# The final norm of the second half of a sequence, done by rows: tiles turned on TensorE behind the last product, the factor as a scalar of each partition

## The chip, the cores and the metric

The kernel runs on one core of one Trainium2 chip. The metric is the device time of one execution in microseconds (us). Engines are named as in the profile: PE is TensorE (PEld its weight loads), DVE is VectorE, ACT is ScalarE, POOL is GpSimd, SP is SyncE, which here only issues DMA transfers.

## What is computed

A decoder layer over 512 positions of 1024 channels: a gated feed-forward block, a mixer of sparse attention and a gated recurrence, a second feed-forward block, each behind an RMS norm and added to the running sum x; then one last RMS norm. The change is in the last block's down projection and in that last norm.

```python
def rmsnorm(x, g):
    x32 = x.astype(jnp.float32)
    y = x32 * lax.rsqrt(jnp.mean(x32 * x32, axis=-1, keepdims=True) + EPS)
    return (y * g.astype(jnp.float32)).astype(x.dtype)

def swiglu(x, w_gate, w_up, w_down):
    return (jax.nn.silu(x @ w_gate) * (x @ w_up)) @ w_down

# ... the last steps of the layer and of the whole:
        x = x + 0.5 * swiglu(rmsnorm(x, ffn2_norm[l]), ffn2_wg[l], ffn2_wu[l], ffn2_wd[l])
    return rmsnorm(x, final_norm)
```

All arrays are float32; the inner width of the feed-forward block is 2816.

## The kernel before

The running sum stands in SBUF turned: eight tiles x[0] to x[7] of 128 channels (partitions) by 512 positions. So a sum over channels goes over partitions and over the eight tiles, and the norm's factor is one number for each column.

A float32 product is made of three products of rounded parts (`mm3`): the high part of the weight with the high and the low part of the activations, and the low part of the weight with the high part. Weight tiles come by DMA as `wr` (queue of SP), ACT rounds them to `wh`, DVE subtracts to get `wl` (`wload`). In a name such as mm<-hh,wh the first tile is written (mm and aux are the two sets of four PSUM buffers each), the second streams through PE, the third stands in it.

`ffn_down` makes x[0] to x[6]: for each, 22 tiles of the hidden layer in three weight chunks (`CHUNKS`: 7, 7 and 8), 66 products over 512 positions, then DVE adds half of the PSUM sum to x[n], and `done(n)` squares it on ACT into `sq` and adds that to `acc` on DVE. For n of 2 and 5 POOL multiplies x[n] in place by the final gain, a column of `vt`.

x[7] is written out by hand behind it. The first two chunks (14 hidden tiles) go over all 512 positions; the last chunk (8 hidden tiles) goes over the two halves of the positions one after the other, `products(0, ...)` and `products(1, ...)`. `squares(h)` adds a half to x[7] and squares it into `last`. `norm_steps` makes the norm's factor for two blocks of 128 positions: PE multiplies `acc` and `last` (standing) with a constant `mean` (streaming), so that the mean square of a position stands on a partition; ACT takes the root (`sd`), DVE the reciprocal (`rs`, one column for each block); PE turns that column, spread over 128 columns, back to a row for all partitions, and ACT copies it to `rstd`. `finish(h, k)` multiplies tile k of a half with the gain's column and with `rstd`: on DVE for k of 0, 1, 3, 4, 6, 7, on POOL for 2 and 5, where the gain is in it already. SP sends the results out, in five transfers for each half (128, 256, 256, 256, 128 KB), in runs of 1 KB.

The order of these last steps on each engine is the order in which they are written (`tc.manual_schedule`). All that goes through the recording helpers carries line L174 in the profile, and all transfers line L162; so the rows are told apart by tile names. L1434 is the end of the program, where every engine drains and waits for the others: four engines count themselves in, POOL counts, and sends all of them on.

Of the kernel before, what the change touches and what calls it, by code (L numbers as in the profile page):

```python
# [9 lines left out]
F32 = mybir.dt.float32  # L10
F32R = mybir.dt.float32r
AF = mybir.ActivationFunctionType
ALU = mybir.AluOpType

P = 128
S = 512
D = 1024
KD = D // P
DFF = 2816
KF = DFF // P  # L20
# [3 lines left out]
QB = 128  # L24
NQ = S // QB
# [8 lines left out]
CHUNKS = ((0, 7), (7, 14), (14, 22))  # L34
# [9 lines left out]
WARM = 8  # L44
HS = S // 2
LEAD = 4
DIRECT = 4


# [6 lines left out]
V_G1, V_GM, V_G2, V_GF = 0, 8, 16, 24  # L56
# [120 lines left out]


@with_exitstack
def hybrid_kernel(ctx, tc, xt, vec, w1u, w1d, wm, wki, wrg, watt, wrnn, wout, w2u, w2d, out):  # L180
    nc = tc.nc
    plan = Plan()
    V, A = plan.engine("DVE", nc.vector), plan.engine("ACT", nc.scalar)
    G, T = plan.engine("POOL", nc.gpsimd), plan.engine("PE", nc.tensor)
    Q = plan.engine("SP", nc.sync)
# [9 lines left out]
    small = ctx.enter_context(tc.tile_pool(name="small", bufs=4))  # L195
# [6 lines left out]
    def nm(s):  # L202
        cnt[0] += 1
        return f"{s}_{cnt[0]}"

    def slot(dt=F32, name="s"):
        return plan.take("slot", big.tile([P, S], dt, tag="slot", name=nm(name)))

    def work(name="t", cols=S):
        return plan.take("tmp", tmp.tile([P, cols], F32, tag="tmp", name=nm(name)))  # L210
# [4 lines left out]
    def psum(tag="mm"):  # L215
        return psp.tile([P, S], F32, tag=tag, name=nm(tag))

    def psaux():
        return psum("aux")

    vt = const.tile([P, NV], F32, name="vt")
    x = [resid.tile([P, S], F32, name=f"x{k}") for k in range(KD)]
    ident = const.tile([P, P], F32, name="ident")
    mean = const.tile([P, P], F32, name="mean")
    epst = const.tile([P, 1], F32, name="epst")
    acc = resid.tile([P, S], F32, name="acc")
    rstd = resid.tile([P, S], F32, name="rstd")

    def col(base, k):
        return vt[:, base + k:base + k + 1]  # L230

    WMAX = KD * P
    def wtiles(cols):
        r = raw.tile([P, WMAX], F32, tag="raw", name=nm("wr"))[:, :cols]
        h = wsp.tile([P, WMAX], F32R, tag="wh", name=nm("wh"))[:, :cols]
        l = wsp.tile([P, WMAX], F32R, tag="wl", name=nm("wl"))[:, :cols]
        return r, h, l

    def wsplit(r, h, l):
        A.activation(h, r, AF.Copy)  # L240
        V.tensor_sub(l, r, f(h))

    def wload(src, cols):
        r, h, l = wtiles(cols)
        Q.dma_start(r, src)
        wsplit(r, h, l)
        return h, l

    def mm3(ps, w, c, y, start, stop):
        h, l = w  # L250
        yh, yl = y
        T.matmul(ps, h[:, c], yh, start=start, stop=False)
        T.matmul(ps, h[:, c], yl, start=False, stop=False)
        T.matmul(ps, l[:, c], yh, start=False, stop=stop)

    def gemm(ps, w, ys, ks, first=True, last=True, m=P, since=0, upto=None):
        n = len(ks)
        for i, k in list(enumerate(ks))[since:upto]:
            mm3(ps, w, slice(i * m, (i + 1) * m), ys[k], first and i == 0, last and i == n - 1)
# [28 lines left out]
    def waits(which, *tiles, aux=0, att=0, slots=0, key=None, mm=0, tmps=0):  # L288
        return which, tiles, aux, att, slots, key, mm, tmps

    def norm_steps(*sums, blocks=range(NQ)):
        pc, n = psaux(), len(blocks)
        for i, a in enumerate(sums):
            if i:
                yield waits("PE", a)
            for j, b in enumerate(blocks):

                T.matmul(pc[:, j * QB:(j + 1) * QB], a[:, b * QB:(b + 1) * QB], mean, start=i + j == 0,
                         stop=i == len(sums) - 1 and j == n - 1)
        yield waits("ACT", pc)  # L300
        sd = small.tile([P, NQ], F32, tag="st", name=nm("sd"))[:, :n]
        A.activation(sd, pc.rearrange("p (b c) -> p b c", c=QB)[:, :n, 0], AF.Sqrt, bias=epst)
        yield waits("DVE", sd)
        rs = small.tile([P, NQ], F32, tag="m8", name=nm("rs"))[:, :n]
        V.reciprocal(rs, sd)
        yield waits("PE", rs)
        pb = psaux()[:, :n * QB]
        for j in range(n):
            T.transpose(pb[:, j * QB:(j + 1) * QB], rs[:, j:j + 1].to_broadcast([P, P]), ident)
        yield waits("ACT", pb)  # L310
        A.activation(rstd[:, blocks[0] * QB:(blocks[-1] + 1) * QB], pb, AF.Copy)

    def norm_rest(steps):
        for _ in steps:
            pass

    lo, hi = slice(0, HS), slice(HS, S)
# [62 lines left out]
    def ffn_up(y, wu, n0, hs, g, waiting=(), given=()):  # L380
# [7 lines left out]
        H = KD // 2 * P  # L388
        f0 = n0 + DIRECT
        count = KF - f0  # L390
# [33 lines left out]
        def together(*steps):  # L424
            steps = list(steps)
            while steps:
                for i in list(steps):
                    try:
                        next(i)
                    except StopIteration:  # L430
                        steps.remove(i)
# [95 lines left out]
        with tc.manual_schedule(engines=ENGINES):  # L527
# [32 lines left out]
            for i in range(len(stream)):  # L560
# [3 lines left out]
                else:  # L564
                    together(results_direct(len(direct) - 1))
                if i + LEAD < len(stream):
                    prepare(i + LEAD)
                else:
                    halve(hs, f0 + i + LEAD - len(stream))
                if i % 14 == 12 and i // 14 < f0:  # L570
# [52 lines left out]
    for k in range(KD):  # L623
        if k:
            Q.dma_start(x[k], xt[k])
        if k % CH == 0:
            c = slice(k * P, (k + CH) * P)
# [14 lines left out]
    for k in range(KD):  # L642
        y.append(norm_tile(k, V_G1, False))
        if k % CH == 0:
            c = slice(k * P, (k + CH) * P)
# [4 lines left out]
    pu, w = psum(), given(AH[0])  # L650
# [3 lines left out]
    hs = []  # L654
# [5 lines left out]
    z, e, s_, s2 = (zt[:, 8 * i:8 * i + 8] for i in range(4))  # L660
# [646 lines left out]
    hs = []  # L1307
    ffn_up(y2, w2u, 0, hs, V_G2)

    def done(n):  # L1310
        sq = acc if n == 0 else work("sq")
        square(n, sq, A)
        if n:
            V.tensor_add(acc, acc, sq)
        if n % 3 == 2:
            G.tensor_scalar(x[n], x[n], col(V_GF, n), 0.0, op0=ALU.mult, op1=ALU.add)

    ffn_down(hs, w2d, done, KD - 1)

    n, e = KD - 1, x[KD - 1]
    po = psum()
    for a, b in CHUNKS[:-1]:
        w = wload(w2d[n, :, a * P:b * P], (b - a) * P)
        gemm(po, w, hs, range(a, b), first=a == 0, last=b == CHUNKS[-1][0])
    V.scalar_tensor_tensor(e, po, 0.5, e, op0=ALU.mult, op1=ALU.add)
    a, b = CHUNKS[-1]
    w = wload(w2d[n, :, a * P:b * P], (b - a) * P)
    last = work("last")  # L1330
    halves = [slice(h * S // 2, (h + 1) * S // 2) for h in range(2)]
    steps = []
    for h in range(2):
        steps.append(norm_steps(acc, last, blocks=(2 * h, 2 * h + 1)))
        next(steps[h])
    pos = [psum()[:, :S // 2] for _ in halves]

    def products(h, i, j):
        for k in range(a + i, min(a + j, b)):
            mm3(pos[h], w, slice((k - a) * P, (k - a + 1) * P), [t[:, halves[h]] for t in hs[k]], k == a, k == b - 1)  # L1340

    def squares(h):
        c = halves[h]
        V.scalar_tensor_tensor(e[:, c], pos[h], 0.5, e[:, c], op0=ALU.mult, op1=ALU.add)
        V.tensor_mul(last[:, c], e[:, c], e[:, c])

    def finish(h, k):
        c = halves[h]
        if k % 2 or k == 0:
            o[h] = slot(F32, "o")  # L1350
        oc = o[h].rearrange("p (k c) -> p k c", k=2)
        dst = oc[:, 1 - k % 2, :]
        if k % 3 == 2:
            G.tensor_mul(dst, x[k][:, c], rstd[:, c])
        else:
            V.scalar_tensor_tensor(dst, x[k][:, c], col(V_GF, k), rstd[:, c], op0=ALU.mult, op1=ALU.mult)
        if k in (0, KD - 1):
            Q.dma_start(out[k][:, c], dst)
        elif k % 2 == 0:
            Q.dma_start(out[k - 1:k + 1, :, c].rearrange("k p c -> p k c"), oc)  # L1360

    o = {}
    with tc.manual_schedule(engines=ENGINES):
        products(0, 0, b)
        squares(0)
        products(1, 0, 3)
        next(steps[0])
        next(steps[0])
        next(steps[0])
        products(1, 3, 5)  # L1370
        next(steps[0])
        norm_rest(steps[0])
        products(1, 5, b)
        finish(0, 0)
        squares(1)
        for k in range(1, 5):
            finish(0, k)
        next(steps[1])
        next(steps[1])
        next(steps[1])  # L1380
        norm_rest(steps[1])
        for k in range(5, KD):
            finish(0, k)
        for k in range(KD):
            finish(1, k)


def _tiles(w, kt, m=P):
# [49 lines left out]
```

## Time and profile before

| | |
|---|---|
| time, median of 3 runs | 1103.74 us (1102.88 to 1103.88) |
| time of the profiled execution | 1102.85 us |
| its span, first to last instruction | 1101.1 us |
| granted TensorE clock, mean | 0.995 |
| busy | PE 98%, PEld 86%, DVE 69%, ACT 54%, POOL 9% |
| read from and written to memory | 130.24 MB, 2.10 MB |

The span is 1.75 us shorter than the profiled execution's own time, and that execution is 0.89 us shorter than the median of the three runs. Times in rows are microseconds from the start of the span. A row of the chain of waits has its start, its length, the engine, the tile written and the count of instructions; a row of a group has count, busy time and mean nanoseconds of one; in brackets stands the engine's idle time before, with what ended it.

### The profile page before, as it was taken

What the parts mean: (1) busy time and instruction counts of PE and PEld (TensorE: products, weight loads), DVE (VectorE), ACT (ScalarE), POOL (GpSimd) and SP (SyncE); (2) the same over time, 40 slices, a digit from 0 to 9 for tenths busy, and PEclk for the clock granted to TensorE, in tenths of its full rate; (3) what the DMA queues carried; (4) which work ended last, traced back from release to release, by engine and by line L of the source; (5) the groups of instructions that cost most, each with busy time, mean ns of one, the idle gap of its engine ahead of it and who ended that gap; (6) DMA issues with size and microseconds to landing.
All of it is one profiled execution on the core that took longest, in us unless ns stands there. A gap on an engine that the chain in (4) does not pass through costs nothing.

```text
span 1101.1 us, 16405 instructions
## 1 busy us (share of the span) xinstructions
PE 1081.7 (98%) x6184; PEld 948.2 (86%) x6184; DVE 764.5 (69%) x1376; ACT 596.1 (54%) x1093; POOL 100.7 (9%) x121
## 2 busy tenths in 40 slices
PE   9999999999999999999999999999999999999995
PEld 7889999998888777888888888888999999988885
DVE  6687777785333778999799868556877777773333
ACT  6665555564222558968885664346655555552220
POOL 0151111100000000000000000003411111000001
PEclk9999999999999999999999999999999999999998
DMA  7396677733333342232232203336967776543322
GB/s 269 83 242 183 159 180 194 162 106 102 102 90 102 116 134 81 83 98 85 77 96 83 81 30 99 112 115 155 218 156 190 191 159 179 122 133 93 96 63 77
DMA packets 61135, 140.22 MB, mean 127 GB/s; under 512 B 7168, under 2 KB 16512, under 8 KB 61056
## 3 DMA queue, kind: packets, MB, share of 16 engines
q1 hardware_dynamic: 45936, 116.58, 33.8%
q0 software_dynamic: 14976, 22.55, 13.4%
q8 instruction: 48, 0.79, 0.3%
q14 instruction: 31, 0.25, 0.1%
q10 hardware_dynamic: 144, 0.05, 0.0%
HBM read 130.24 MB, written 2.10 MB: 120 GB/s over the span
## 4 chain that ended last, share of the span: by engine, by line
PE 79%; DVE 9%; ACT 6%; DMA 3%; issue 3%; SPq 0%; DVEq 0%; ACTq 0%
PE mm L174 55%; PE aux L174 24%; DVE wl L174 3%; ACT wh L174 3%; DVE s L174 1%; DMA a<-w1u 1%; DMA gr<-wrg 1%; DVE tg L174 1%; ACT hh L174 1%; DVE yl L174 1%; ACT tg L174 0%; SPq L162 0%; DVE yf L174 0%; DMA wr<-w1u 0%; ACT cm L174 0%
## 5 line engine op out<-in xcount | busy, mean ns | idle before, releaser
L174 DVE TENSOR_TENSOR wl<-wr,wh 128x1024 fp32r<-128x1024 f32 (+3 forms) x204 | 193.0, 955 | 115.4 <-ACT wh L174 115.0
L174 ACT ACTIVATE wh<-wr 128x1024 fp32r<-128x1024 f32 (+4 forms) x206 | 171.2, 835 | 177.7 <-PE mm L174 67.1
L174 PE MATMUL mm<-cm,wh 128*128 128x256 f32 x1088 | 200.4, 284 | 2.5 <-ACT tg L174 2.5
L174 PEld LDWEIGHTS mm<-cm,wh 128*128 128x128 f32 x1088 | 169.7, 192 | 4.9 <-ACT tg L174 4.8
L174 PE MATMUL mm<-yh,wh 128*128 128x512 f32 (+1 forms) x416 | 164.7, 397 | 1.4 <-ACT yh L174 0.6
L174 PE MATMUL mm<-yl,wh 128*128 128x512 f32 (+1 forms) x416 | 163.3, 393 | 0.8 <-DVE yl L174 0.8
L174 PE MATMUL mm<-yh,wl 128*128 128x512 f32 x408 | 159.9, 392 | 0.0
L174 PE MATMUL mm<-cm,wl 128*128 128x256 f32 x544 | 153.9, 283 | 0.0
L174 PE MATMUL aux<-cm,wh 128*128 128x256 f32 x816 | 150.0, 283 | 0.0
L174 ACT ACTIVATE wh<-s 128x512 fp32r<-128x512 f32 x136 | 81.9, 626 | 101.7 <-DVE s L174 69.9
L174 DVE TENSOR_TENSOR wl<-s,wh 128x512 fp32r<-128x512 f32 x136 | 93.7, 690 | 52.9 <-ACT wh L174 50.6
L174 PEld LDWEIGHTS aux<-cm,wh 128*128 128x128 f32 x816 | 127.3, 192 | 0.0
L174 PE MATMUL aux<-cm,wl 128*128 128x256 f32 x408 | 115.5, 283 | 0.0
L174 PEld LDWEIGHTS mm<-cm,wl 128*128 128x128 f32 x544 | 104.3, 192 | 0.0
L174 PEld LDWEIGHTS mm<-yh,wh 128*128 128x128 f32 (+1 forms) x416 | 78.3, 188 | 19.2 <-ACT yh L174 1.9
L174 PEld LDWEIGHTS mm<-yl,wh 128*128 128x128 f32 (+1 forms) x416 | 78.0, 187 | 17.3 <-DVE yl L174 2.2
L174 PEld LDWEIGHTS mm<-yh,wl 128*128 128x128 f32 x408 | 77.0, 189 | 16.6 <-DVE wl L174 0.3
L174 PE MATMUL mm<-hh,wh 128*128 128x512 f32 (+1 forms) x206 | 78.8, 382 | 0.0
L174 PE MATMUL mm<-hl,wh 128*128 128x512 f32 (+1 forms) x206 | 78.5, 381 | 0.0
L174 PE MATMUL mm<-hh,wl 128*128 128x512 f32 (+1 forms) x206 | 78.4, 381 | 0.0
L174 PEld LDWEIGHTS aux<-cm,wl 128*128 128x128 f32 x408 | 78.3, 192 | 0.0
L174 PE MATMUL aux<-hh,wl 128*128 128x512 f32 x154 | 60.0, 390 | 0.0
(207 smaller groups left out, 1893.3 us busy)
## 6 DMA issues: line engine op xcount, KB each, us to landing
wr<-wm SPq DMA_DIRECT2D x39, 512.0 KB, 3.6
wr<-w2u SPq DMA_DIRECT2D x26, 512.0 KB, 3.7
wr<-w1u SPq DMA_DIRECT2D x21, 512.0 KB, 4.6
s<-w2u SPq DMA_DIRECT2D x36, 256.0 KB, 4.6
s<-w2u POOLq DMA_DIRECT2D x36, 256.0 KB, 5.4
s<-w1u SPq DMA_DIRECT2D x32, 256.0 KB, 5.1
s<-w1u POOLq DMA_DIRECT2D x32, 256.0 KB, 5.4
wr<-w1d SPq DMA_DIRECT2D x16, 448.0 KB, 3.3
```

What stands on the lines that cost most here:

```text
L174: return call(*args, **kw)
```

## The change

The two halves of the positions are finished in two ways. `lo` is positions 0 to 255, `hi` is 256 to 511.

- x[0] to x[6] are multiplied by the final gain in place by ACT, after they are squared; POOL has no step in the norm any more.
- For x[7], 10 hidden tiles go over all 512 positions (`APART`), and 12 over the halves, one after the other. All three weight chunks are loaded ahead of them.
- `lo` is finished as before, with all of its multiplications on DVE, and goes out as a channel-by-position block. Six of its eight tiles stand ahead of `squares(hi, ...)` on DVE, two behind.
- `hi` is turned: behind the last product, PE turns x[0] to x[6] and the scaled x[7] in blocks of 128 by 128 (16 `transpose`, each with the identity streaming) into four PSUM tiles of 128 positions by 512 channels. The products of `last` with `mean` stand after the tenth. The reciprocal of the root (`rs`, two columns) is then the scalar of each partition: DVE and ACT each empty two of the PSUM tiles with it into `ot`.
- Four transfers of 256 KB in runs of 2 KB bring `ot` out, three on SP's queue and one on ACT's. The output is one array of two halves; the first half is transposed and the two are joined on the host.

```diff
@@ constants @@
+APART = 10
@@ hybrid_kernel @@
-def hybrid_kernel(ctx, tc, xt, ..., w2d, out):
+def hybrid_kernel(ctx, tc, xt, ..., w2d, both):
+    out = both[0].rearrange("(k p c) -> k p c", k=KD, p=P)
+    turned_out = both[1].rearrange("(j p c) -> j p c", j=2, p=P)
@@ -1312,77 +1316,91 @@
         square(n, sq, A)
         if n:
             V.tensor_add(acc, acc, sq)
-        if n % 3 == 2:
-            G.tensor_scalar(x[n], x[n], col(V_GF, n), 0.0, op0=ALU.mult, op1=ALU.add)
+        A.activation(x[n], x[n], AF.Copy, scale=col(V_GF, n))
 
     ffn_down(hs, w2d, done, KD - 1)
 
 
 
+
     n, e = KD - 1, x[KD - 1]
-    po = psum()
-    for a, b in CHUNKS[:-1]:
+    po, ws = psum(), []
+    for a, b in CHUNKS:
         w = wload(w2d[n, :, a * P:b * P], (b - a) * P)
-        gemm(po, w, hs, range(a, b), first=a == 0, last=b == CHUNKS[-1][0])
+        ws += [(w, i) for i in range(b - a)]
+        for k in range(a, min(b, APART)):
+            mm3(po, w, slice((k - a) * P, (k - a + 1) * P), hs[k], k == 0, k == APART - 1)
     V.scalar_tensor_tensor(e, po, 0.5, e, op0=ALU.mult, op1=ALU.add)
-    a, b = CHUNKS[-1]
-    w = wload(w2d[n, :, a * P:b * P], (b - a) * P)
-    last = work("last")
-    halves = [slice(h * S // 2, (h + 1) * S // 2) for h in range(2)]
-    steps = []
-    for h in range(2):
-        steps.append(norm_steps(acc, last, blocks=(2 * h, 2 * h + 1)))
-        next(steps[h])
-    pos = [psum()[:, :S // 2] for _ in halves]
-
-    def products(h, i, j):
-        for k in range(a + i, min(a + j, b)):
-            mm3(pos[h], w, slice((k - a) * P, (k - a + 1) * P), [t[:, halves[h]] for t in hs[k]], k == a, k == b - 1)
-
-    def squares(h):
-        c = halves[h]
-        V.scalar_tensor_tensor(e[:, c], pos[h], 0.5, e[:, c], op0=ALU.mult, op1=ALU.add)
+    last, scaled = work("last"), work("eg")
+    steps = norm_steps(acc, last, blocks=(0, 1))
+    next(steps)
+    pc = psaux()
+    for j in range(2):
+        T.matmul(pc[:, j * QB:(j + 1) * QB], acc[:, (2 + j) * QB:(3 + j) * QB], mean, start=j == 0, stop=False)
+    pos = [psum()[:, :HS] for _ in range(2)]
+
+    def products(h, a, b):
+        for k in range(a, b):
+            w, i = ws[k]
+            mm3(pos[h], w, slice(i * P, (i + 1) * P), [t[:, (lo, hi)[h]] for t in hs[k]], k == APART, k == KF - 1)
+
+    def squares(c, ps):
+        V.scalar_tensor_tensor(e[:, c], ps, 0.5, e[:, c], op0=ALU.mult, op1=ALU.add)
         V.tensor_mul(last[:, c], e[:, c], e[:, c])
 
-    def finish(h, k):
-        c = halves[h]
+    def finish(k):
         if k % 2 or k == 0:
-            o[h] = slot(F32, "o")
-        oc = o[h].rearrange("p (k c) -> p k c", k=2)
+            o.append(slot(F32, "o"))
+        oc = o[-1].rearrange("p (k c) -> p k c", k=2)
         dst = oc[:, 1 - k % 2, :]
-        if k % 3 == 2:
-            G.tensor_mul(dst, x[k][:, c], rstd[:, c])
+        if k < KD - 1:
+            V.tensor_mul(dst, x[k][:, lo], rstd[:, lo])
         else:
-            V.scalar_tensor_tensor(dst, x[k][:, c], col(V_GF, k), rstd[:, c], op0=ALU.mult, op1=ALU.mult)
+            V.scalar_tensor_tensor(dst, x[k][:, lo], col(V_GF, k), rstd[:, lo], op0=ALU.mult, op1=ALU.mult)
         if k in (0, KD - 1):
-            Q.dma_start(out[k][:, c], dst)
+            Q.dma_start(out[k], dst)
         elif k % 2 == 0:
-            Q.dma_start(out[k - 1:k + 1, :, c].rearrange("k p c -> p k c"), oc)
-
-    o = {}
+            Q.dma_start(out[k - 1:k + 1].rearrange("k p c -> p k c"), oc)
+
+    turned = {}
+
+    def turn(k, j, src):
+        if k % 4 == 0:
+            turned[j, k // 4] = psum(("mm", "aux")[j == 1 and k == 4])
+        T.transpose(turned[j, k // 4][:, k % 4 * QB:(k % 4 + 1) * QB], src[:, (2 + j) * QB:(3 + j) * QB], ident)
+
+    o = []
     with tc.manual_schedule(engines=ENGINES):
-        products(0, 0, b)
-        squares(0)
-        products(1, 0, 3)
-        next(steps[0])
-        next(steps[0])
-        next(steps[0])
-        products(1, 3, 5)
-        next(steps[0])
-        norm_rest(steps[0])
-        products(1, 5, b)
-        finish(0, 0)
-        squares(1)
-        for k in range(1, 5):
-            finish(0, k)
-        next(steps[1])
-        next(steps[1])
-        next(steps[1])
-        norm_rest(steps[1])
-        for k in range(5, KD):
-            finish(0, k)
-        for k in range(KD):
-            finish(1, k)
+        products(0, APART, KF)
+        squares(lo, pos[0])
+        products(1, APART, APART + 3)
+        for _ in range(3):
+            next(steps)
+        products(1, APART + 3, APART + 5)
+        norm_rest(steps)
+        products(1, APART + 5, KF)
+        for k in range(KD - 2):
+            finish(k)
+        squares(hi, pos[1])
+        for k in range(KD - 2, KD):
+            finish(k)
+        A.activation(scaled[:, hi], e[:, hi], AF.Copy, scale=col(V_GF, n))
+        for k, j in [(k, j) for j in range(2) for k in range(KD - 1)]:
+            if (k, j) == (3, 1):
+                for i in range(2):
+                    T.matmul(pc[:, i * QB:(i + 1) * QB], last[:, (2 + i) * QB:(3 + i) * QB], mean, start=False, stop=i == 1)
+            turn(k, j, x[k])
+        for j in range(2):
+            turn(n, j, scaled)
+        sd, rs = (small.tile([P, NQ], F32, tag=t, name=nm("sd"))[:, :2] for t in ("st", "m8"))
+        A.activation(sd, pc.rearrange("p (b c) -> p b c", c=QB)[:, :2, 0], AF.Sqrt, bias=epst)
+        V.reciprocal(rs, sd)
+        ot = [slot(F32, "ot") for _ in range(4)]
+        for j in range(2):
+            V.tensor_scalar(ot[2 * j], turned[j, 0], rs[:, j:j + 1], None, op0=ALU.mult)
+            A.activation(ot[2 * j + 1], turned[j, 1], AF.Copy, scale=rs[:, j:j + 1])
+            for i in range(2):
+                (A if i and j else Q).dma_start(turned_out[j, :, i * S:(i + 1) * S], ot[2 * j + i])
 
 
 def _tiles(w, kt, m=P):
@@ kernel @@
-    args.append(nc.dram_tensor("out", (KD, P, S), F32, kind="ExternalOutput").ap())
+    args.append(nc.dram_tensor("out", (2, D * S // 2), F32, kind="ExternalOutput").ap())
...
-    return np.ascontiguousarray(r.results[0]["out"].reshape(D, S).T)[None]
+    first, second = r.results[0]["out"].reshape(2, D * S // 2)
+    return np.concatenate([first.reshape(D, HS).T, second.reshape(HS, D)])[None]
```

In the built program the other instructions of all engines stand in the order of before, PE's up to the tenth hidden tile of x[7]; ACT has one table load, ahead of the first root, as before; POOL's last instructions are the two transfers into tiles named s at the end of the second block's up projection, and then its drain.

More of the change, by code (lines that the diff above doesn't have):

```diff
@@ L179, in hybrid_kernel @@
 @with_exitstack
-def hybrid_kernel(ctx, tc, xt, vec, w1u, w1d, wm, wki, wrg, watt, wrnn, wout, w2u, w2d, out):
+def hybrid_kernel(ctx, tc, xt, vec, w1u, w1d, wm, wki, wrg, watt, wrnn, wout, w2u, w2d, both):
     nc = tc.nc
+    out = both[0].rearrange("(k p c) -> k p c", k=KD, p=P)
+    turned_out = both[1].rearrange("(j p c) -> j p c", j=2, p=P)
     plan = Plan()
```

## The prediction

> **What bounds the kernel now.** First the page's busy shares, then the chain of waits over the last 40 us, then the last transfer and the end of the program.
>
> ```profile
> PE 1081.7 (98%) x6184; PEld 948.2 (86%) x6184; DVE 764.5 (69%) x1376; ACT 596.1 (54%) x1093; POOL 100.7 (9%) x121
> ```
>
> PE bounds the whole, so 1.0 us off PE's work or off the tail behind it is 1.0 us off the time, and anything else is worth nothing while PE covers it. The chain shows where PE stops being the bound:
>
> ```profile
> 1081.98 3.95 PE mm L174 x33
> 1085.93 0.61 PE aux L174 x4
> 1086.54 0.71 PE mm L174 x6
> 1087.25 0.28 PE aux L174 x2
> 1087.52 1.09 PE mm L174 x9
> ...
> 1088.63 0.44 DVE x L174
> ...
> 1089.09 0.92 DVE last L174
> 1090.01 1.19 DVE o L174 x3
> ...
> 1091.33 0.45 PE aux L174 x2
> ...
> 1091.80 0.39 ACT rstd L174
> ...
> 1092.22 1.05 DVE o L174
> 1093.27 0.86 DVEq L1434
> 1094.13 1.58 DVE o L174 x4
> ```
>
> The last product ends at 1088.61. Behind it stand 7.1 us of small steps to 1095.71, two thirds of them (1.19 + 1.05 + 0.86 + 1.58) multiplications of tiles on DVE. What follows is in the issues of SP, the landing times of the tile out, and the rows of the program's end:
>
> ```profile
> 1095.96 0.45 SPq L162 DMA_DIRECT2D out<-o  x1
> DMA to landing us min/median/max: 1.7/2.2/2.9
> L1434 SPq EVENT_SEMAPHORE  x9: 27/28/28, 1096.5 to 1098.3; - x9
> L1434 POOLq DRAIN  x1: 8040/8040/8040, 1092.2 to 1092.2; - x1
> L1434 DVEq DRAIN  x1: 3524/3524/3524, 1092.2 to 1092.2; - x1
> L1434 POOLq EVENT_SEMAPHORE  x2: 17/17/17, 1100.3 to 1100.4; - x2
> 1092.26 1.58 POOL L174 TENSOR_TENSOR o<-x,rstd 128x256 f32<-128x256 f32 x2 [2.54 <-ACT rstd L174]
> 943.67 1.75 POOL L162 DMA_DIRECT2D s<-w2u  x2 [8.18 <-DVE wl L174]
> ```
>
> This is the row to stop at. The last transfer is issued at 1095.96 and SP sees its landing at 1098.3, 2.3 us on. But the program doesn't go on then: POOL's drain runs from 1092.2 for 8.04 us, to 1100.3, and only then does POOL count the others in. DVE's drain ends at 1095.7, with DVE's last multiplication; POOL's last multiplication ends at 1092.26 + 1.58 = 1093.84, and its drain goes on for 6.4 us. So the end (span 1101.1) is 0.8 us of barrier behind POOL, and SP was ready 2.0 us before.
>
> **Before the last product.** Twelve products over 512 columns become 24 over 256.
>
> ```profile
> 1056.61 24.48 PE mm L174 x108
> ```
>
> These are 108 at 0.2267 us; the 33 above, of the narrow form, took 0.1197 each. So 24 x 0.1197 - 12 x 0.2267 = +0.15: the last product ends at 1088.77. The first half's products end 1.28 earlier (36 x 0.1197 less 24 x 0.1197 and 12 x 0.2267), and so does all that hangs on them, its factor among it.
>
> ACT gets seven scalings of 128x512 during the down projection:
>
> ```profile
> 1061.22 0.95 ACT L174 ACTIVATE wh<-wr 128x896 fp32r<-128x896 f32 x1 [3.22 <-issue]
> L174 ACT ACTIVATE yh<-x,vt 128x512 fp32r<-128x512 f32 x24 | 17.1, 711 | 1.6 <-DMA vt<-vec 1.5 <-DMA x<-xt 0.2
> ```
>
> Each costs about 0.71 and lies in the 3.22 us that ACT idles ahead of the next weight chunk, behind the square: nothing. Without that cover it would be 7 x 0.71 = 5.0 us on PE's weights. The last one delays ACT's table load by as much; the first root, which waits for the first half's products, comes far behind both. POOL's two scalings go; nobody waited for them.
>
> **The first half's multiplications** move wholly to DVE, with six ahead of the second half's squares.
>
> ```profile
> 1087.98 0.48 DVE L174 SCALAR_TENSOR_TENSOR o<-x,vt,rstd 128x256 f32<-128x256 f32 x1 [0.94 <-ACT rstd L174]
> 1089.94 1.27 DVE L174 SCALAR_TENSOR_TENSOR o<-x,vt,rstd 128x256 f32<-128x256 f32 x3
> 1085.35 0.42 DVE L174 TENSOR_TENSOR last<-x 128x256 f32<-128x256 f32 x1
> ```
>
> The first starts at 1087.98 - 1.28 = 1086.70. Three with the gain's column took 1.27, a step of 0.40; the form without a column takes 0.42 against 0.48, so I take 0.34. Six end their turn at 1088.74, or at 1089.1 at 0.40. PE's last product is there at 1088.77, so queuing them ahead costs 0 to 0.3; I take 0.
>
> **The second half behind the last product.** The half's sum on DVE (0.44) ends at 1089.25. The square took 0.92 while a POOL multiplication ran beside it and 0.42 (row above) with POOL idle; with POOL gone I take 0.42: `last` is ready at 1089.7.
>
> Meanwhile PE turns tiles. The nearest row is the attention's turning, in the same form, four at a time:
>
> ```profile
> 657.90 0.60 PE L174 MATMUL aux<-ident,pm 128*128 128x128 f32 x4
> 1090.07 0.71 PE L174 MATMUL aux<-mean,last 128*128 128x128 f32 x4 [1.47 <-DVE last L174]
> 1090.82 0.26 ACT L174 ACTIVATE sd<-aux,epst 128x2 f32<-128x2 f32 x1 [2.87 <-PE aux L174]
> 1091.12 0.15 DVE L174 RECIPROCAL rs<-sd 128x2 f32<-128x2 f32 x1
> L174 DVE SCALAR_TENSOR_TENSOR x<-mm,x 128x512 f32<-128x512 f32 x17 | 11.8, 691 | 41.3 <-PE mm L174 41.3
> L174 ACT ACTIVATE xc<-mm,vt 128x512 f32<-128x512 f32 x8 | 6.2, 778 | 9.2 <-PE mm L174 9.2
> ```
>
> Four in 0.60 are a step of 0.11. Ten from 1088.77 end at 1089.9, 0.2 behind `last`: a new, small wait, with the root, the reciprocal and all evictions behind it. From there the old chain's steps: the root starts 0.75 later (1090.65), the reciprocal 0.30 after it, and ends at 1091.1. The six tiles left on PE are turned by 1091.2, so the reciprocal and the last turned tile come together. The way back to a row (0.45 on PE), the copy to rstd (0.39) and six of DVE's multiplications (1.05 + 0.86 + 1.58) are gone.
>
> In their place stand four evictions of 128x512 out of PSUM with a column. No row has DVE's form; the two nearest, one on each engine, say 0.69 and 0.78, and I take each for its engine, with 0.1 either way. DVE is done at 1091.85 and 1092.5, ACT at 1092.0 and 1092.75.
>
> **The transfers.** The first half's last two tiles leave DVE by 1090.5; their 384 KB take 1.1 us at the rate below and 1.3 of start and receipt, so they are through near 1092.9 and hold up no more than the first bytes of what follows. Issues cost 0.45 on SP: 1091.9, 1092.3, 1092.7, and ACT's at 1092.75. The low bound is the last issue plus the median landing: 1092.75 + 2.2 = 1094.95. But four transfers of 256 KB, 1.05 MB, come within 0.9 us, and a view of the stretches has what the output can take:
>
> ```profile
> 1091.50:1094.00 2.50, 0.26 (x2) 0.02 (x1) 2.34 (x4) 0.38 (x1) 1.58 (x2) 0.83 1.03 342
> 1089.25:1089.75 0.50, 0.00 (x0) 0.00 (x0) 0.50 (x1) 0.00 (x0) 0.48 (x1) 1.00 0.74 252
> 1054.00:1055.00 1.00, 1.00 (x6) 0.84 (x5) 0.00 (x0) 0.00 (x0) 0.00 (x0) 1.00 0.86 111
> ```
>
> The last two columns are the busy share of the DMA engines and GB/s. With results alone going out, the engines were full (1.03) at 342 GB/s. The shortest transfer (128 KB, 1.7) is 0.4 of that and 1.3 of start and receipt. So: 1091.9 + 1.3 + 1.05 MB / 342 GB/s = 1091.9 + 1.3 + 3.1 = 1096.3. This I take, 2.0 before 1098.3. The Trainium skill (DMA: Bandwidth & Descriptors, Bandwidth) lists 6.15 us for 1 MB, read from memory through POOL's queue; by that the sum would be 3.1 us worse, but the row above moved 0.86 MB of results in 2.5 us, so the trace doesn't bear it out for these stores.
>
> **The end.** POOL's last instructions are now the two transfers at 943.67 to 945.42. If its drain takes the same 6.4 to 8.0 us, it is over before 954, and SP's landing sets the end: a further 2.0 us. The sum: 1096.3 + 0.8 = 1097.1 against a span of 1101.1, that is -4.0. From the profiled execution's 1102.85 this gives 1098.9; from the median 1103.74, which I forecast, 1099.7.
>
> **The rivals.** (1) POOL's drain is no work of POOL's own but something that comes at the end in any case, about 2.0 behind the last landing. For it: no row shows what POOL does in it. Against it: SP, ACT and DVE drain with their last work, and SP was done at 1098.3. Then only -2.0 is left: 1101.7, just inside what 0.2% (2.2 us, about what a measurement of this kernel can tell from no change) allows. The Trainium skill (VectorE: DVE Perf Modes, The DRAIN you can't avoid) has the drains around a program at about 12 ns, the same on all five engines; by that POOL's is no cost of its multiplications and this rival holds, but 8040 ns in the row disagrees.
>
> (2) The stores start slowly or run below the full rate, as in the half microsecond at 252 GB/s, or at half of 342: 4.2 or 6.1 us in place of 3.1, so 1100.8 or 1102.7.
>
> (3) Slower than before: the four stores, now bunched on two queues in runs of another length, hit what the load at 1054 hit, engines 0.86 busy at 111 GB/s. At that rate 1.05 MB take 9.4 us: 1099.7 + 6.4 = 1106.1. It costs the whole gain from 148 GB/s downwards (1.05 MB in 3.1 + 4.0). Against it: that row is a load's start while no row of results is under 252 with the engines busy.
>
> **How the numbers follow.** The forecast gets 0.72, rival 1 0.15, rival 2 0.09, rival 3 0.04. The range: at the bottom the low bound of the landing, 1.3 less, 1098.4, and 0.3 for the evictions and steps: 1098.1. At the top rival 1 with the runs' spread: 1101.9. Rival 1 lies on the bound of 0.2%, a fifth of it beyond; rival 2 is half beyond. Faster: 0.72 + 0.03 + 0.05 = 0.80; within 0.2%: 0.16; slower: 0.04. Without rival 1 the range would be 1098.1 to 1101.
>
> **What would show it.** In the new profile: POOL's drain near 945, and SP's last landing directly ahead of POOL's events; the last product near 1088.8; the first eviction near 1091.2 and the last near 1092.7; DMA at a share of 1.0 for three us from about 1092.8. Wrong would be: a POOL drain that still ends 2 us behind SP; roots that start after 1091.5 because turning steps are longer than 0.11; a DMA rate under 300 GB/s in that stretch; or PE waiting for weights between 1010 and 1078, which would mean that ACT's scalings weren't covered.

## The result, and the profile after

The changed kernel takes 1098.44 us (median of 6 runs, 1097.67 to 1098.91); the kernel before, on the same chip, 1102.97 (6 runs, 1102.27 to 1103.88). The ratio is 0.9957, with a 95% interval of 0.9944 to 0.997: 4.5 us less, where 4.0 were forecast (1099.7, from a median of 1103.74). The profiled execution took 1097.67 us.

The head of the page after, answering to the shares shown of before:

```profile
span 1095.7 us, 16454 instructions
PE 1081.9 (99%) x6210; PEld 949.7 (87%) x6210; DVE 762.0 (70%) x1374; ACT 602.5 (55%) x1102; POOL 93.8 (9%) x115
```

PE's work is what it was (1081.7 before); its share rises because the span ends sooner. The chain of waits over the last microseconds (start, length, what), after:

```profile
1085.11 3.60 PE mm L175 x31
1088.70 0.60 PE aux L175 x4
1089.30 0.11 PE mm L175
1089.41 0.33 PE aux L175 x3
1089.74 0.12 PE mm L175
1089.86 0.04 issue
1089.90 0.75 DVE ot L175
1090.65 0.66 DVEq L1452
```

Before, the chain behind the last product went DVE, PE, ACT, DVE, with two thirds of it multiplications. Now the view keeps it on PE as far as the last turned tile (1089.86), and one eviction follows. By the program, though, DVE's first eviction reads a PSUM tile that the first ten turns have filled; what it needs is the reciprocal, which ends at 1089.80 in the rows below. The last turned tile is there within 0.05 us of that, so both ways end together. The same stretch in the timeline of each engine (start, length, engine, operation, count, what it waited for):

```profile
1087.33 0.28 PE L175 MATMUL mm<-hh,wl 128*128 128x256 f32 x1
1087.45 1.25 PE L175 MATMUL mm<-ident,x 128*128 128x128 f32 x10
1088.59 0.71 PE L175 MATMUL aux<-mean,last 128*128 128x128 f32 x4
1089.57 0.27 PE L175 MATMUL mm<-ident,eg 128*128 128x128 f32 x1
1085.56 2.10 DVE L175 TENSOR_TENSOR o<-x,rstd 128x256 f32<-128x256 f32 x6 [0.94 <-ACT rstd L175]
1087.65 0.42 DVE L175 SCALAR_TENSOR_TENSOR x<-mm,x 128x256 f32<-128x256 f32 x1
1088.11 0.42 DVE L175 TENSOR_TENSOR last<-x 128x256 f32<-128x256 f32 x1
1089.34 0.26 ACT L175 ACTIVATE sd<-aux,epst 128x2 f32<-128x2 f32 x1 [0.72 <-PE aux L175]
1089.63 0.17 DVE L175 RECIPROCAL sd<-sd 128x2 f32<-128x2 f32 x1 [0.37 <-ACT sd L175]
1089.90 1.41 DVE L175 TENSOR_SCALAR ot<-mm,sd 128x512 f32<-128x512 f32 x2
1089.89 0.69 ACT L175 ACTIVATE ot<-mm,sd 128x512 f32<-128x512 f32 x1 [0.29 <-PE mm L175]
1090.48 0.68 ACT L175 ACTIVATE ot<-aux,sd 128x512 f32<-128x512 f32 x1
1090.68 1.32 SPq L163 DMA_DIRECT2D out<-ot  x3
1091.19 0.35 ACTq L163 DMA_DIRECT2D out<-ot  x1
```

The first row is the last product; it ends at 1087.33 + 0.28 = 1087.61. Everything from here on is counted from that end, for each run from its own row, since the executions reach it at different times. The program's end after, with POOL's last work (POOL's timeline, the rows of the end, and the landing times of the tile ot):

```profile
941.20 1.75 POOL L163 DMA_DIRECT2D s<-w2u  x2 [7.53 <-DMA s<-w2u]
L1452 POOLq DRAIN  x1: 10340/10340/10340, 942.0 to 942.0; - x1
L1452 SPq EVENT_SEMAPHORE  x4: 28/28/28, 1094.2 to 1094.8; - x4
L1452 POOLq EVENT_SEMAPHORE  x2: 17/17/17, 1095.0 to 1095.1; - x2
DMA to landing us min/median/max: 2.1/2.8/3.2
```

POOL's drain starts at 942.0, takes 10.34 us and is over at 952.3. The last store is issued at 1091.60 and lands 3.2 us later, at 1094.8; SP sees it there, and POOL counts the others in at 1095.0, directly behind it. Before, it did so at 1100.3, 2.0 behind SP.

The last product of before, for the same count:

```profile
1088.32 0.28 PE L174 MATMUL mm<-hh,wl 128*128 128x256 f32 x1
```

It ends at 1088.60. So, in us behind the last product:

| | last DVE or ACT step ends | last landing | POOL's drain ends | end of span |
|---|---|---|---|---|
| before | 7.12 | 9.67 | 11.67 | 12.46 |
| after | 3.70 | 7.15 | long done | 8.12 |

The stretch behind the last product is 4.34 us shorter: the landing comes 2.5 earlier, and the end lies 0.97 behind the landing, not 2.79, which is 1.82. That is the measured gain, within the interval (0.3% to 0.56%, 3.3 to 6.2 us). The two profiled spans differ by more, about 5.3; the last product came 1.0 earlier in this one execution. The windows at 393 us (length, busy time and count of each engine, granted clock, DMA share, GB/s), before:

```profile
393.00:397.00 4.00, 3.77 (x10) 2.95 (x10) 1.47 (x3) 2.24 (x3) 0.00 (x0) 0.57 0.70 224
```

and after:

```profile
393.00:397.00 4.00, 3.77 (x17) 3.10 (x17) 1.90 (x4) 2.25 (x3) 0.00 (x0) 1.00 0.71 221
```

At equal busy time PE issued 10 matmuls against 17, at a granted clock of 0.57 against 1.00. It isn't the change: the fifth and the sixth experiment, which alter only the stores of the changed kernel, have 0.62 and 0.57 there. Nor does this clock alone decide when the last product comes: the fourth and the tenth have 1.00 there as well and end it at 1089.44 and 1088.82, and why executions reach it at different times stays open. The spans of the 53 runs of the kernel before that stand beside the experiments have a mean of 1100.85, those of the 11 runs of the changed kernel (these 6 and 5 of the last experiment) 1096.56: 4.3 apart, what the stretch behind the last product lost. On the chip of the last experiment, which has both, they are 1101.12 (9 runs) and 1096.78 (5 runs), 4.34 apart.

### The profile page after: what moved, and what is told of

It reads as the page before. It is cut to its first block, busy times and chain, and to the rows that moved or that the text cites. A ratio compares the mean times of both kernels' runs of the same rounds, so it can differ in the third digit from the quotient of the medians.

```text
span 1095.7 us, 16454 instructions
## 1 busy us (share of the span) xinstructions
PE 1081.9 (99%) x6210; PEld 949.7 (87%) x6210; DVE 762.0 (70%) x1374; ACT 602.5 (55%) x1102; POOL 93.8 (9%) x115
## 4 chain that ended last, share of the span: by engine, by line
PE 79%; DVE 8%; ACT 5%; DMA 4%; issue 3%; SPq 1%; DVEq 0%; ACTq 0%; POOL 0%; POOLq 0%
PE mm L175 55%; PE aux L175 24%; DVE wl L175 3%; ACT wh L175 2%; DMA a<-w1u 2%; DVE s L175 2%; DMA gr<-wrg 1%; SPq L163 1%; DVE tg L175 1%; DVE yl L175 1%; DMA cm<-cb 1%; ACT hh L175 1%; DVE yf L175 0%; DMA s<-w1u 0%; DVE ca L175 0%
```

## The experiments

The theory: the end is set by the later of two things, the last landing and POOL's drain, which is over 6.4 us behind POOL's last step; the change brought the one forward by 2.5 us and took the other away, which gave 1.8 more. Against it: the drain belongs to the program's end (rival 1); or the gain is one, and POOL's part only the slower DVE beside it. One table for all ten, in us behind each run's last product, with the ratio to the kernel before on the same chip; the text then goes through them.

| run | last step | last landing | POOL's last step ends | its drain ends | end of span | median us | ratio (95%) |
|---|---|---|---|---|---|---|---|
| e1_no_pool | 6.92 | 9.38 | (none) | long done | 10.28 | 1100.58 | 0.9981 (0.9972 to 0.999) |
| e2_pool_at_factor | 3.70 | 7.15 | 2.66 | 9.09 | 9.86 | 1100.70 | 0.9982 (0.9973 to 0.9991) |
| e3_pool_at_eviction | 3.70 | 7.16 | 4.26 | 10.68 | 11.46 | 1102.85 | 1.0003 (0.9994 to 1.0012) |
| e4_pool_first_half | 4.04 | 7.50 | -0.16 | 6.26 | 8.46 | 1099.32 | 0.9972 (0.996 to 0.9983) |
| e5_half_stores | 3.70 | 6.05 | (none) | long done | 7.01 | 1097.29 | 0.9951 (0.9936 to 0.9967) |
| e6_short_runs | 3.70 | 7.55 | (none) | long done | 8.51 | 1099.13 | 0.9971 (0.9961 to 0.9982) |
| e7_early_store | 3.83 | 7.07 | (none) | long done | 7.97 | 1099.06 | 0.997 (0.9959 to 0.9982) |
| e8_split_at_14 | 5.06 | 8.51 | (none) | long done | 9.47 | 1099.45 | 0.9974 (0.9963 to 0.9984) |
| e9_early_store_2 | 3.83 | 7.07 | (none) | long done | 7.98 | 1098.78 | 0.9959 (0.9945 to 0.9972) |
| e10_changed_again | 3.71 | 7.16 | (none) | long done | 8.12 | 1099.01 | 0.9962 (0.995 to 0.9975) |

**e1_no_pool: POOL's part of the change alone.** The kernel before, with POOL's scalings and multiplications in the final norm given to DVE.

```diff
-        if n % 3 == 2:
-            G.tensor_scalar(x[n], x[n], col(V_GF, n), 0.0, op0=ALU.mult, op1=ALU.add)
...
-        if k % 3 == 2:
-            G.tensor_mul(dst, x[k][:, c], rstd[:, c])
-        else:
-            V.scalar_tensor_tensor(dst, x[k][:, c], col(V_GF, k), rstd[:, c], op0=ALU.mult, op1=ALU.mult)
+        V.scalar_tensor_tensor(dst, x[k][:, c], col(V_GF, k), rstd[:, c], op0=ALU.mult, op1=ALU.mult)
```

> The kernel before, with POOL out of the norm and nothing else changed: its two scalings go, and its four multiplications of 128x256 are made on DVE with the gain's column. Theory A (POOL's drain is a cost of its own that starts when POOL's last step is done, and the end of the program waits for it): DVE has two more multiplications in each half (0.8 us) but none of its steps runs beside a POOL step (0.5 + 0.6 + 0.4 us back), so the last landing moves by 0 to -0.3; POOL's drain lies near 942 and the end follows SP's landing within 1.0 us instead of 2.8. Time 1.9 to 2.2 us under the kernel before; last product to end of span 10.3 to 10.6 us instead of 12.4. Rival B (something comes about 2 us behind the last landing whatever POOL did): 0 to -0.3 us, last product to end 12.2.

POOL's last work and the end of the program:

```profile
943.82 1.76 POOL L162 DMA_DIRECT2D s<-w2u  x2 [10.06 <-DVE s L174]
L1429 SPq EVENT_SEMAPHORE  x11: 17/28/28, 1096.0 to 1098.7; - x11
L1429 POOLq EVENT_SEMAPHORE  x4: 17/17/17, 1098.1 to 1098.7; - x4
L1429 POOLq DRAIN  x3: 40/93/10958, 944.5 to 1098.5; - x3
```

The long drain (10.96 us) now starts at 944.5, and POOL's events come at 1098.1, 0.2 behind the landing at 1088.52 + 9.38 = 1097.9. Nothing else of the end was touched, so the drain is POOL's own and rival 1 falls. DVE, which took over POOL's steps, was even done a little earlier (6.92 against 7.12), and the landing came 0.29 earlier (9.38 against 9.67): a slower DVE beside POOL explains no more of the gain than that. The span ends 2.18 sooner behind the last product than before, the median is 2.1 below the kernel before: half of the change's gain, from code that the turning doesn't need.

**e2_pool_at_factor and e3_pool_at_eviction: POOL put back late.** The changed kernel, with one POOL step of 128x128 whose output nobody reads, once behind the reciprocal and once behind DVE's second eviction.

```diff
+    junk = work("junk")[:, :QB]
...
         V.reciprocal(rs, sd)
+        G.tensor_scalar(junk, acc[:, :QB], rs[:, 0:1], 0.0, op0=ALU.mult, op1=ALU.add)
```

```diff
+            if j:
+                G.tensor_scalar(junk, ot[2][:, :QB], rs[:, 0:1], 0.0, op0=ALU.mult, op1=ALU.add)
             for i in range(2):
```

> The changed kernel with one small POOL step added (128x128, result unused) that waits for the reciprocal, so it runs at about 2.4 us behind the last product, some 0.5 us long. Theory A: POOL's drain ends 6.4 us behind that step, 9.2 to 9.4 us behind the last product, where SP was ready at 7.3: the span gets 1.8 to 2.1 us longer, time +1.9. Rival B: the step lies beside the evictions and costs nothing, 0 to +0.1 us.

> The same small POOL step, but waiting for DVE's second eviction, 1.5 us later than in the run before this one. Theory A: the end moves with the step, +1.5 us on the run with the step at the factor, +3.3 to +3.6 us on the changed kernel. If the drain had a fixed end or ran by a clock of its own since the program's start, both places would cost the same. Rival B: 0 to +0.1 us.

POOL's step and the drain of the former:

```profile
1091.19 0.37 POOL L175 TENSOR_SCALAR junk<-acc,sd 128x128 f32<-128x128 f32 x1 [145.73 <-DVE sd L175]
L1454 POOLq EVENT_SEMAPHORE  x4: 17/17/17, 1098.0 to 1098.7; - x4
L1454 POOLq DRAIN  x3: 40/93/6857, 1091.1 to 1098.5; - x3
```

and of the latter:

```profile
1092.41 0.37 POOL L175 TENSOR_SCALAR junk<-ot,sd 128x128 f32<-128x128 f32 x1 [147.64 <-DVE ot L175]
L1455 POOLq EVENT_SEMAPHORE  x4: 17/17/17, 1099.2 to 1099.9; - x4
L1455 POOLq DRAIN  x3: 40/102/6842, 1092.4 to 1099.7; - x3
```

Read the drain's length and first start together: 1091.13 + 6.86 = 1098.0, 6.43 behind the end of the step (1091.56), and 1092.36 + 6.84 = 1099.2, 6.42 behind 1092.78. The landing is where the changed kernel has it (7.15 and 7.16). The step comes 1.60 later in the second than in the first, and so does the end (11.46 against 9.86): the end follows POOL's last step us for us. Against the changed kernel the tail is 1.74 longer with the step at the factor (1.8 to 2.1 expected) and 3.34 longer with the step at the eviction (3.3 to 3.6 expected): one step of 0.37 us, read by nobody, gives back 3.34 of the 4.34. The median time, 1102.85 against 1102.67 of the kernel before on that chip, shows nothing left of the gain, while the mean of the spans is still 0.7 shorter (1100.19 against 1100.87); that difference lies outside the span, and no trace shows what it is.

**e4_pool_first_half: POOL back where the drain is hidden.** The changed kernel with two of the first half's multiplications on POOL, as before.

```diff
-        if k < KD - 1:
+        if k % 3 == 2:
+            G.tensor_mul(dst, x[k][:, lo], rstd[:, lo])
+        elif k < KD - 1:
             V.tensor_mul(dst, x[k][:, lo], rstd[:, lo])
```

> The changed kernel with POOL's share of the first half put back: tiles 2 and 5 of the first half are multiplied on POOL, beside DVE, and are done about when the last product ends. Theory A: POOL's drain ends 6.4 us behind them, 0.3 to 1 us before SP sees the last landing, so it is hidden: the time is that of the changed kernel within 0.3 us. Rival C (any POOL step in the norm costs about 1.9, wherever it stands): +1.9 us. A slower DVE beside POOL could add up to 0.3 in either theory.

POOL, DVE and the drain:

```profile
1087.43 1.85 POOL L175 TENSOR_TENSOR o<-x,rstd 128x256 f32<-128x256 f32 x2 [142.66 <-ACT rstd L175]
1087.38 2.52 DVE L175 TENSOR_TENSOR o<-x,rstd 128x256 f32<-128x256 f32 x4 [0.94 <-ACT rstd L175]
1089.83 0.41 DVE L175 SCALAR_TENSOR_TENSOR x<-mm,x 128x256 f32<-128x256 f32 x1
L1454 POOLq DRAIN  x3: 40/93/8313, 1087.4 to 1097.6; - x3
```

POOL's steps end at 1089.28 and the drain at 1087.39 + 8.31 = 1095.7, again 6.4 behind them, but 1.24 before the landing: it costs nothing. What remains is 0.34, and the DVE rows have it: four multiplications, partly beside POOL, take 2.52, where the changed kernel did six in 2.10, so the second half's sum starts 0.39 behind the last product (1089.44) and not 0.04. That is the price of sharing with POOL here, a fifth of the drain's.

**e5_half_stores and e6_short_runs: the last transfers.** The former stores only half of each tile of the second half, so half of that output is left out; the latter writes the same bytes in runs of 1 KB in place of 2 KB.

```diff
-                (A if i and j else Q).dma_start(turned_out[j, :, i * S:(i + 1) * S], ot[2 * j + i])
+                (A if i and j else Q).dma_start(turned_out[j, :, i * S:i * S + HS], ot[2 * j + i][:, :HS])
```

```diff
-    turned_out = both[1].rearrange("(j p c) -> j p c", j=2, p=P)
+    turned_out = both[1].rearrange("(j i a p c) -> j i p a c", j=2, i=2, a=2, p=P)
...
+                (A if i and j else Q).dma_start(turned_out[j, i], ot[2 * j + i].rearrange("p (a c) -> p a c", a=2))
```

> The changed kernel storing only the first 256 of each 512 columns of the four turned tiles (half of the second half's output is left out); all other steps stay. Theory A (the last four stores are bound by the rate of the DMA engines, 1.05 MB in 2.7 us, so what counts is bytes): half the bytes land 1.0 to 1.4 us sooner, until the last issue plus 1.7 to 2.2 us is the bound; last product to end 6.7 to 7.1 us instead of 8.1. Rival B (the last store's own issue, start and receipt set the landing): 0 to -0.2 us.

> The changed kernel with the second half written in runs of 1 KB instead of 2 KB, the same bytes in the same four stores. Theory A (rate goes with the length of a run: the kernel before wrote 1 KB runs at 342 GB/s, the changed kernel 2 KB runs at 381 to 393): the four stores take 3.1 us instead of 2.7, the end comes 0.3 to 0.4 us later, last product to end 8.5. Rival B (the rate differs because nothing else, or another bank of memory, is written at that time): 0 to +0.1 us.

The windows of the stores (the last two columns are the DMA share and GB/s), of the changed kernel, of whose 1.05 MB all but 0.02 lie in the first of them:

```profile
1091.50:1094.25 2.75, 0.00 (x0) 0.00 (x0) 0.00 (x0) 0.00 (x0) 0.00 (x0) 1.00 1.00 373
1092.00:1092.50 0.50, 0.00 (x0) 0.00 (x0) 0.00 (x0) 0.00 (x0) 0.00 (x0) 1.00 1.04 393
1093.50:1094.00 0.50, 0.00 (x0) 0.00 (x0) 0.00 (x0) 0.00 (x0) 0.00 (x0) 1.00 1.02 381
1094.00:1094.50 0.50, 0.00 (x0) 0.00 (x0) 0.00 (x0) 0.00 (x0) 0.00 (x0) 1.00 0.61 230
```

and of the short runs, then of the half stores:

```profile
1093.00:1095.25 2.25, 0.00 (x0) 0.00 (x0) 0.00 (x0) 0.00 (x0) 0.00 (x0) 0.50 1.03 346
1092.50:1094.50 2.00, 0.00 (x0) 0.00 (x0) 0.00 (x0) 0.00 (x0) 0.00 (x0) 0.80 0.79 262
```

The engines are full in the changed kernel and with the short runs, at 373 to 393 GB/s in runs of 2 KB and 346 in runs of 1 KB. From the first to the last packet of the four stores in the trace it is 2.89 us after (1091.52 to 1094.41, 363 GB/s) and 3.24 with the short runs (324 GB/s): 0.35 of the 0.40 us by which the landing moved. So the stores' rate does set the end of the changed kernel, and the run length their rate. Half the bytes bring the landing 1.10 earlier, as theory A has it, but there the rate no longer binds alone: the engines are busy to 0.79 over the window, the stores take 1.78 us where 0.52 MB at 346 GB/s would take 1.52, and the last landing comes 2.06 behind its issue, in the expectation's bound of 1.7 to 2.2.

**e7_early_store and e9_early_store_2: a version that might be better.** DVE's first eviction in two pieces, each stored as soon as it is there, so that the train starts earlier; e9 lets the full tile of ACT go ahead of the second piece.

```diff
-        for j in range(2):
-            V.tensor_scalar(ot[2 * j], turned[j, 0], rs[:, j:j + 1], None, op0=ALU.mult)
...
+        for c in (lo, hi):
+            V.tensor_scalar(ot[0][:, c], turned[0, 0][:, c], rs[:, 0:1], None, op0=ALU.mult)
+            Q.dma_start(turned_out[0, :, c], ot[0][:, c])
+        Q.dma_start(turned_out[0, :, S:], ot[1])
```

```diff
+        V.tensor_scalar(ot[0][:, lo], turned[0, 0][:, lo], rs[:, 0:1], None, op0=ALU.mult)
+        Q.dma_start(turned_out[0, :, lo], ot[0][:, lo])
+        Q.dma_start(turned_out[0, :, S:], ot[1])
+        V.tensor_scalar(ot[0][:, hi], turned[0, 0][:, hi], rs[:, 0:1], None, op0=ALU.mult)
+        Q.dma_start(turned_out[0, :, hi], ot[0][:, hi])
```

> The changed kernel with DVE's first eviction in two pieces of 256 columns, each stored at once, so that the first store is issued 0.33 us sooner; one store more. If the DMA engines' rate bounds the end (theory A), the whole train of stores moves with its first: -0.2 to -0.35 us, last product to end 7.8 to 7.9. If SP's issues bind (rival B), the extra issue of 0.4 to 0.45 us makes it +0.1 to +0.4.

> As the run with the early store, but SP issues ACT's first tile ahead of DVE's second piece, so that the train of stores has no gap behind its first 128 KB. Theory A (the end goes with the train): last product to end 7.75 to 7.9 us against 8.1 of the changed kernel and 7.97 of the early store; time 0.2 to 0.35 us under the changed kernel of the same call, less than its runs differ among themselves. Rival B (issues bind): no better than the early store, 7.95 to 8.1.

Both expected more than they got. The first store is issued 0.26 earlier than in the changed kernel (2.81 behind the last product against 3.07), but the last landing comes only 0.08 earlier (7.07) and the end 0.14 to 0.15; e9 is no better than e7, as its rival B has it. The median of e9 (1098.78, 1097.58 to 1099.07) isn't told apart from the changed kernel's on the same chip (1099.01, 1098.13 to 1099.35). The windows of e9 show what happened to the head start:

```profile
1093.00:1093.25 0.25, 0.00 (x0) 0.00 (x0) 0.00 (x0) 0.00 (x0) 0.00 (x0) 1.00 0.69 221
1093.25:1095.50 2.25, 0.00 (x0) 0.00 (x0) 0.00 (x0) 0.00 (x0) 0.00 (x0) 0.54 1.03 376
```

The small first piece is nearly through before the next one arrives (share 0.69), since SP issues the second store 0.44 us behind the first and 128 KB take about 0.35 at the rate of the row behind; from there on the engines are full. e7 has the same gap, at 0.62 in its window from 1093.50 to 1093.75. So SP's issues and the rate bind in turn, and neither theory had it whole.

**e8_split_at_14: the place of the split.** More of the last tile's products run over all 512 columns, which leaves fewer narrow ones behind the first half.

```diff
-APART = 10
+APART = 14
```

> The changed kernel with the halves of the last tile split as before, 14 hidden tiles over all positions and 8 over the halves. The first half's factor then comes 1.4 us later against the last product, and DVE's six multiplications, which stand ahead of the second half's squares, end 1.4 us behind the last product instead of with it. Theory A (the earlier split is what hides the first half's finish): +1.2 to +1.4 us, last product to end 9.4 to 9.5. Rival B (the split is worth only its products, 0.05 us for each hidden tile): -0.1 to -0.2 us.

DVE, and the wait of the statistic on PE:

```profile
1088.42 2.10 DVE L175 TENSOR_TENSOR o<-x,rstd 128x256 f32<-128x256 f32 x6 [0.94 <-ACT rstd L175]
1090.43 0.42 DVE L175 SCALAR_TENSOR_TENSOR x<-mm,x 128x256 f32<-128x256 f32 x1
1091.37 0.71 PE L175 MATMUL aux<-mean,last 128*128 128x128 f32 x4 [1.25 <-DVE last L175]
```

The six multiplications now end 1.49 behind the last product (1089.03), the second half's sum starts 1.40 behind it, and PE waits 1.25 us for `last`, which it doesn't in the changed kernel. The end is 1.35 later. So the split at 10 has just enough cover: there the multiplications end within 0.05 us of the last product.

**e10_changed_again: the changed kernel, unaltered, beside e9.**

> The changed kernel once more, unaltered, to have its time beside the early store on the same chip. Every theory: 4.2 us under the kernel before by its tail (12.4 to 8.1 us), with up to 1 us either way from where PE waits for data in the middle of the program; last product to end 8.1 us again, since no step of the tail depends on that.

The stretch behind the last product repeats to 0.01 us (7.16 and 8.12); the time, 1099.01, is 4.0 below the kernel before (1103.02).

## Why the prediction was right

**The two halves of the sum.** Forecast: 2.0 from the landing and 2.0 from POOL's drain. Measured behind the last product: 2.5 (where the forecast comes to 2.2, its last product being 0.15 later) and 1.8. Neither stands alone, because the later one sets the end: e1, with the drain gone and the old landing, gains 2.18 of the 4.34; e3, with the new landing and a late drain, 1.00 (12.46 to 11.46), and nothing in the time; the two together, 4.34. How the 2.5 of the landing divide among the parts of the change is only in part shown. One part left out at a time costs the landing 0.40 (runs of 2 KB, e6) and 1.36 (the split at 10, e8), and taking POOL out of the kernel before brought 0.29 (e1). No run has the split at 10 without the turning, so what the turning brings by itself stays open. Rival 1 (the drain comes with the program's end) falls with e1 to e3: it goes with POOL's own last step. The Trainium skill's rule beside it (VectorE: DVE Perf Modes, The DRAIN you can't avoid), some 12 ns on all engines, is contradicted by POOL's 6842 to 10958 ns, the more so since the end moves with them.

**The stores: the term that was mis-sized.** The prediction took 342 GB/s from results in runs of 1 KB, so 3.1 us; the runs after are 2 KB long, and the stores take 2.89. The landing came 7.15 behind the last product, where 1096.3 - 1088.77 = 7.5 was forecast. Of the 0.35 between them 0.18 is the rate, 0.11 start and receipt (0.84 from the first issue to the first packet and 0.35 from the last packet to the landing, where 1.3 were taken), and 0.06 the earlier issue. e6, with runs of 1 KB, measures 7.55. Rivals 2 and 3 (252 and 111 GB/s) did not come: the first half microsecond with the engines full is at 393. The Trainium skill's 6.15 us for 1 MB (DMA: Bandwidth & Descriptors, Bandwidth), a figure for loads, isn't what these stores take, 2.89 us for 1.05 MB.

**The chain behind the last product.** The sum on DVE starts 0.04 behind it, so queuing lo's six multiplications (2.10 us, 0.35 each) ahead cost what was taken, nothing; e8 prices the cover when it is gone. `last` is ready 0.92 behind it (0.93 forecast). The "new, small wait" of 0.2 for the turning did not show: the step was right (1.14 from the first of ten turns to the statistic behind them, 0.11 each), but PE begins the first turn 0.12 behind the start of the last product, not at its end, and so the statistic starts at 1088.59, 0.06 behind `last`. The reciprocal ends 2.2 behind the last product (2.33 forecast). The evictions of 128x512 took 0.75 each on DVE (1.41 for two, as the second starts before the first has ended) and 0.69 on ACT, where 0.69 and 0.78 were forecast. The first store is issued 3.07 behind the last product (3.13 forecast).

**Before the last product.** ACT's scalings are covered, with this row of its timeline after:

```profile
1060.04 0.95 ACT L175 ACTIVATE wh<-wr 128x896 fp32r<-128x896 f32 x1 [2.41 <-PE mm L175]
```

ACT still idles 2.41 us there, against 3.22 before: 0.8 less, about one scaling (0.73 here), and no wait of PE is listed between 1010 and 1078, the stretch that the prediction named. The 0.15 us for the narrow products can't be read: the last product of the kernels with the split at 10 ends anywhere from 1087.61 to 1089.51, that of before and e1 at 1088.5 to 1088.6.

**The end.** From the last product to the end of the span 8.3 us were forecast (1097.1 - 1088.77) and 8.12 measured: the landing came 0.35 sooner, and what follows it takes 0.97 where 0.8 was put. That the medians fell by 4.5 on the first chip and 4.0 on the last is within what executions differ by ahead of 1085 us; why they do stays open, beyond the clock at 393.

## What to carry to other kernels

Ask of every engine not only when its last result is read but when it is done with the program: here a step of 0.37 us on POOL that nobody reads put back 3.34 of the 4.34 us that the rewriting of the tail had taken off, and giving POOL's last steps to DVE gained 2.18 with no other change (e1). As far ahead of the final landing as in e4 (drain over 1.24 us before it), a step on POOL costs nothing at the end. Take a transfer's rate from a row with the same run length, and a tail's steps from the start of the instruction ahead, not its end, where an engine pipelines. Compare tails from a common event, such as the last product, when executions reach it up to 2 us apart.

## What the runs showed of the hardware

- POOL's drain at the end of the program is over 6.41 to 6.43 us behind POOL's last arithmetic step, whatever that was (0.37 us over 128x128 or 1.6 to 1.9 over two of 128x256; the kernel before, e2, e3 and e4). Where its last work was a DMA issue it was over 8.6 to 9.8 us behind that; what POOL does meanwhile no trace shows.
- Stores of results with the DMA engines full moved 339 to 346 GB/s in runs of 1 KB (the kernel before and e6) and 373 to 393 in runs of 2 KB (the changed kernel).
- DVE's multiplications of two tiles, 0.35 us each alone (2.10 for six), took 0.63 on average where two of POOL's ran beside them (2.52 for four, e4).
- The granted clock falls to 0.57 to 0.74 at 393 us in some executions and stays at 1.00 in others of kernels that are the same up to there; what decides it stays open.
